# A hybrid decoder layer on one core: weight splits, bank choice and the second norm's sums at the borders of the up-projection

## The chip, the core and the metric

The kernel runs on one NeuronCore of a Trainium2 chip. The metric is the device time of one execution in microseconds (us). Before the change it is 923.74 us, the median of three runs (923.59 to 923.84).

The engines are TensorE (PE, with its weight loads listed as PEld), VectorE (DVE), ScalarE (ACT), GpSimd (POOL) and SyncE (SP), which issues most transfers. Matmuls write to PSUM, which has eight banks. A bank holds 512 fp32 values in each of 128 partitions.

## The reference, cut to what matters

One layer of a decoder, 1024 tokens of width 1024, in fp32:

```
z = rms_norm(h, norm_mix_g);  proj = z @ w_in            # pooling and recurrent heads follow
h = h + concat([y_pool, y_lru]) @ w_out
z = rms_norm(h, norm_mlp_g)                              # the second norm
h = h + square(relu(z @ w_up)) @ w_down                  # the MLP, 1024 -> 4096 -> 1024
z = rms_norm(h, norm_ple_g)
gate = sigmoid(z @ w_ple_gate + b_ple_gate)
h = h + gate * (p @ w_ple_proj)
return rms_norm(h, norm_final_g)
```

rms_norm divides by the root of the mean square over the 1024 channels and multiplies by a gain.

## The kernel before

**Products.** Channels lie on partitions, so the 1024 channels are eight tiles of 128, and tokens lie along the free dimension in two halves of 512. Every fp32 operand is split into a high part `hi` (rounded to fp32r) and the rest `lo`; `split` writes `hi` on ACT (line 185, or 188 with a gain) and `lo` on DVE (186, or 189). A product is three matmuls: hi by hi, hi by lo, lo by hi (line 363, in `mm`).

**The up-projection** is done in 16 pairs m = 0 to 15 by a seven-product scheme (P1 to P7) that combines quarter blocks of the weights and of the activations. Each product is 12 matmuls: four tiles t of the operand by three. P6 and P7 read the tiles `a` of indices 0 to 3, P4 and P5 those of indices 4 to 7, P1, P2 and P3 the tiles `y`. The operands with t = 3 need the last out-projection result (o = 7), so `up_first` runs t = 0 to 2 of P6, P7, P4, P5, and then their t = 3.

**Weights** are asked for through one list, `todo`. `ask()` takes the next entry, issues its loads and its split, and appends the result to `asked`; `weights()` asks once more and hands out the oldest. The up-projection's weights use four half-megabyte buffers in turn, so the fifth split has to wait until the matmuls of the first are done.

**The second norm.** `norm.acc` (T[4]) collects the squares of the eight tiles. `casts` splits it to `hl` tiles (420 on ACT, 421 on DVE); `sums` sends each half's hi and lo through a matmul with a matrix of ones (434, 435), and `rstd` makes 1/rms of the result (459 to 465). This is called inside pair m = 1, and pair 0 is finished by `finish_up` after it. The last norm of the kernel uses `folded` instead: rows 64 to 127 are copied by ACT beside rows 0 to 63 and added, hi goes to rows 0 to 63 of one tile and lo to rows 64 to 127, and one matmul with ones sums both (444 to 451).

**PSUM** is given out in two shapes: `bank` (four single banks, pool pd) and `banks` (two tiles of two banks, pool pp). `mlp_bank` and `psum` count their calls in `turn`: `mlp_bank` takes the two-bank shape at each third call, and `ple_psum`, in the gate stage, takes it at each odd count and otherwise two single banks, one for the gate `ps_e` and one for the projection `ps_j`. With the two-bank shape both halves are one tile, named `ps_e`.

**The end of the up-projection** is `up_last` (pair 15). It opens the down-projection's tiles, runs P4, P6, P7, and calls `prepare(0, tp)` for the four operand tiles of the first down product, which are splits of X[tp] into `a` on ACT and DVE.

**The last stage** works token by token in four groups of 128 tokens (i = 0 to 3). `gate_opened(i)` runs the gate's first matmul (1243) and adds the bias in PSUM on DVE (1252); `token_proj(i)` is six matmuls of the projection (1267); `token_gate(i)` is the other 23 of the gate, with the next group's first matmul after eleven of them. Tokens of the second half are transposed through DRAM (`turn` and `late`, lines 1198 to 1212) meanwhile.

**Order.** A scheduler in the framework orders each engine's instructions at build time, except those that are pinned by `pin` and `keep_in_program_order`. Each engine then runs its list in order.

Of the kernel before, what the change touches and what calls it, by code (L numbers as in the profile page):

```python
# [18 lines left out]
HALF = 512  # L19
# [44 lines left out]
def block_kernel(  # L64
# [67 lines left out]
    def bank(name):  # L132
        return pd.tile([P, HALF], F32, tag="pd", name=name)
# [19 lines left out]
    def f32(ap):  # L153
        return ap.bitcast(F32)
# [6 lines left out]
    def got(ps):  # L161
        if ps.shape[-1] > HALF:
            return ps.rearrange("p (b j a) -> p b a j", b=2, a=2)
        return ps.rearrange("p (j a) -> p a j", a=2)
# [177 lines left out]
    asked = []  # L342

    def ask():
        if todo:
            fn, *args = todo.pop()
            asked.append(fn(*args))

    def weights():
        ask()  # L350
        return asked.pop(0)
# [37 lines left out]
    class Norm:  # L389
# [47 lines left out]
                parts.append((hs, o))  # L437
            return parts

        def folded(self, hs, t):  # L440

            rows = self.acc[:, hs]
            x = rows[:64]
            nc.scalar.activation(t[:64], rows[64:], AF.Copy)
            nc.vector.tensor_tensor(x, x, t[:64], ALU.add)
            both, _ = self.parts(hs)
            hi, lo = (by(both[n], both) for n in (slice(0, 64), slice(64, P)))
            nc.vector.tensor_copy(hi, got(x))
            nc.vector.tensor_tensor(lo, got(x), f32(hi), ALU.subtract)
            o = bank(f"{self.name}_ps{hs.start}")  # L450
            nc.tensor.matmul(o, ones, turns(both), start=True, stop=True)
            return [(hs, o)]
# [355 lines left out]
    def mlp_bank(name):  # L808
        turn.append(name)
        return banks(name)[:, :HALF] if len(turn) % 3 == 0 else bank(name)  # L810
# [48 lines left out]
    leave("y2")  # L859
    *E, u0, u1 = space("wu", 4, F32, "right")  # L860
    up_spare += u0, u1
    for o in range(0, NT, 2):
        t = o // 2
        for i in range(2):
            split(H[o + i][:, FIRST], *half(B[t], i), col("g_mlp", o + i))
# [11 lines left out]
    def take(to, ps, y):  # L877

        nc.vector.tensor_tensor(by(to, ps), got(ps), by(y, ps), ALU.subtract)

    def up_first():
        cc, c11, c12, c21, c22 = up_sums(0)
        ps, ws = {}, {}
        ask()
        for kind in FIRST_UP[:4]:
            ws[kind], ps[kind] = weights(), mlp_bank(f"ps_{kind}_u0")
            up_product(0, kind, ps[kind], range(3), ws[kind])
        for kind in FIRST_UP[:4]:
            up_product(0, kind, ps[kind], range(3, 4), ws[kind])
        ws["P1"] = weights()  # L890
        with tc.issue_after(up_lower[0, "P1"]):
            up_second(NT - 1)
            norm.tmp = T[2:3]
            norm.add(H[NT - 1])
            copy(c22, ps["P5"])
            norm.casts()
        for kind in FIRST_UP[4:6]:
            ps[kind] = mlp_bank(f"ps_{kind}_u0")
            up_product(0, kind, ps[kind], w=ws.get(kind))
        up_product(0, "P3", ps["P5"], more=True)  # L900
        copy(c11, ps["P1"])
        take(c12, ps["P6"], c11)
        add_got(c21, ps["P7"], c12)
        add_got(c11, ps["P2"])
        dv(ALU.subtract, c22, c21, c22)
        add_got(c21, ps["P4"])
        take(c12, ps["P5"], c12)
# [22 lines left out]
    def up_pair(m):  # L930
        cc, c11, c12, c21, c22 = up_sums(m)
        a, d = up_open(m)
        b = chains[m]
        if m > 1:
            up_fourth(m - 1)()
        else:
            norm.rstd(R, norm.sums(cast=True))
            leave("hl")
        up_product(m, "P6", b, more=True)
        copy(c12, b)  # L940
        up_product(m, "P2", a, more=True)
        copy(c11, a)
        up_product(m, "P3", d, more=True)
        take(c12, d, c12)
        if m == 1:
            finish_up(0, up_sums(0)[0])()
        up_product(m, "P7", b, more=True)
        take(c22, b, c22)

    def up_last():  # L950
        m = NPAIR - 1
        cc, c11, c12, c21, c22 = up_sums(m)
        preload_down()
        a, d = up_open(m)
        store_up = up_fourth(m - 1)
        up_product(m, "P2", a, more=True)
        copy(c11, a)
        up_product(m, "P3", d, more=True)
        first = open_down()
        with tc.issue_after(first):  # L960
            store_up()
        ps = bank(f"ps_P4_u{m}")
        up_product(m, "P4", ps)
        load_w(0, 0, 3)
        copy(c21, ps)
        ps = bank(f"ps_P6_u{m}")
        up_product(m, "P6", ps)
        prepare(0, 0)
        take(c12, ps, c12)
        dv(ALU.subtract, c22, c12, c22)  # L970
        add(c21, c12)
        take(c12, d, c12)
        ps = banks(f"ps_P7_u{m}")[:, :HALF]
        up_product(m, "P7", ps)
        for tp in range(1, NQ):
            prepare(0, tp)
        add_both(cc[:, 1].rearrange("p (y s) -> p y s", y=2), ps)

    chains = {}

# [515 lines left out]
```

## Time and profile before

| | |
|---|---|
| median of three runs | 923.74 us (923.59 to 923.84) |
| the profiled execution's own time | 923.41 us |
| its span, first to last instruction | 921.6 us |
| busy: PE, PEld, DVE, ACT, POOL | 911.9, 792.9, 701.7, 468.9, 38.0 us |
| matmuls | 4227 |
| granted TensorE clock, mean | 0.998 |
| transfers | 142.46 MB, mean 155 GB/s |

Times in the views are us from the start of the span. A row of the timeline merges instructions of one kind that follow each other: start, length, engine, line, operation, output and input tiles, count, and in brackets the idle time before it with what ended it. The time outside the span is 923.41 - 921.6 = 1.8 us.

### The profile page before, as it was taken

The page shows a single profiled execution, that of the slowest core. Times are in us where ns is not written, and L with a number is a line of the kernel's source. Part 1 is how long each engine was busy: PE and PEld are TensorE (multiplying, and loading weights), DVE is VectorE, ACT ScalarE, POOL GpSimd, SP SyncE. Part 2 cuts the span into 40 slices and gives each one's busy share as a digit, 9 for nine tenths or more (in the row PEclk, how much of TensorE's full clock was granted, in tenths as well). Part 3 has the DMA queues.
Part 4 walks back from the last instruction along what each step waited for, and adds up shares of the span by engine and source line. Part 5 has one row for each costly group of instructions (what it writes and reads, how often), then busy time and mean ns, then how long its engine had stood idle before and what let it go on. Part 6 is the DMA issues. An engine that isn't in the chain of part 4 may idle for free.

```text
span 921.6 us, 11220 instructions
## 1 busy us (share of the span) xinstructions
PE 911.9 (99%) x4227; PEld 792.9 (86%) x4227; DVE 701.7 (76%) x850; ACT 468.9 (51%) x606; POOL 38.0 (4%) x54
## 2 busy tenths in 40 slices
PE   9999999999999999999999999999999999999996
PEld 7888888888888888888888888888888888888885
DVE  7998984668877566656766889899876679798766
ACT  6568992447554444445444654354343436656323
POOL 3400001000000000000000000000000000000001
PEclk9999999999999999999999999999999999999999
DMA  7211055214478767876864997466633351031453
GB/s 272 100 47 41 28 181 143 76 46 111 109 196 230 208 164 212 223 202 170 239 199 161 359 324 275 134 199 201 199 119 107 114 161 46 1 125 59 114 171 116
DMA packets 56870, 142.46 MB, mean 155 GB/s; under 512 B 4976, under 2 KB 9968, under 8 KB 56816
## 3 DMA queue, kind: packets, MB, share of 16 engines
q1 hardware_dynamic: 54080, 132.84, 44.2%
q0 software_dynamic: 2736, 8.91, 5.7%
q8 instruction: 33, 0.54, 0.3%
q14 instruction: 21, 0.17, 0.1%
HBM read 106.08 MB, written 35.65 MB: 154 GB/s over the span
## 4 chain that ended last, share of the span: by engine, by line
PE 93%; DVE 3%; issue 1%; DMA 1%; ACT 0%; SPq 0%; DVEq 0%; POOLq 0%; POOL 0%
PE ps_P_d L363 31%; PE ps_b_u L363 12%; PE ps_i L363 9%; PE ps_a_u L363 8%; PE ps_d_u L363 8%; PE ps_o L363 8%; PE ps_e L363 8%; PE ps_l L363 3%; PE ps_P_u L363 1%; PE ps_l L570 1%; PE ps_j L363 1%; DVE y L189 1%; PE ps_g L639 1%; PE ps_e L1243 1%; PE ps_p L363 1%
## 5 line engine op out<-in xcount | busy, mean ns | idle before, releaser
L363 PE MATMUL ps_P_d<-a,wd_P_hi 128*128 128x512 f32 x880 | 261.8, 379 | 0.0
L363 PEld LDWEIGHTS ps_P_d<-a,wd_P_hi 128*128 128x128 f32 x880 | 166.4, 189 | 23.5
L363 PE MATMUL ps_P_d<-a,wd_P_lo 128*128 128x512 f32 x440 | 166.8, 379 | 0.0
L363 PE MATMUL ps_b_u<-a,wu_P 128*128 128x512 f32 x504 | 113.5, 379 | 0.0
L363 PEld LDWEIGHTS ps_b_u<-a,wu_P 128*128 128x128 f32 x504 | 95.3, 189 | 13.5
L363 PEld LDWEIGHTS ps_P_d<-a,wd_P_lo 128*128 128x128 f32 x440 | 83.2, 189 | 11.8
L363 PE MATMUL ps_a_u<-y,wu_P 128*128 128x512 f32 x360 | 82.6, 379 | 0.0
L363 PEld LDWEIGHTS ps_a_u<-y,wu_P 128*128 128x128 f32 x360 | 68.1, 189 | 9.6
L820 DVE TENSOR_TENSOR t_h<-t_h,ps_P_d 128x512 f32<-128x512 f32 (+1 forms) x56 | 42.4, 758 | 36.7 <-PE ps_P_d L363 36.7
L186 DVE TENSOR_TENSOR a<-wd,a 128x1024 fp32r<-128x1024 f32 x56 | 67.0, 1217 | 0.9 <-ACT a L185 0.6
L363 PE MATMUL ps_i<-a,wi_hi 128*128 128x512 f32 x256 | 66.2, 381 | 0.0
L363 PE MATMUL ps_o<-y,wo_hi 128*128 128x512 f32 x256 | 65.7, 379 | 0.0
L185 ACT ACTIVATE a<-wd 128x1024 fp32r<-128x1024 f32 x56 | 57.9, 1048 | 7.0 <-PE ps_P_d L363 7.0
L363 PEld LDWEIGHTS ps_i<-a,wi_hi 128*128 128x128 f32 x256 | 48.1, 189 | 7.9 <-issue 1.0
L185 ACT ACTIVATE wd_P_hi<-wd 128x1024 fp32r<-128x1024 f32 x24 | 25.3, 1056 | 57.3 <-PE ps_P_d L363 57.2
L363 PEld LDWEIGHTS ps_o<-y,wo_hi 128*128 128x128 f32 x256 | 48.4, 189 | 6.8
L838 DVE SCALAR_TENSOR_TENSOR t_h<-t_h,rstd 128x2048 f32<-128x2048 f32 x16 | 36.7, 2291 | 19.3 <-ACT t_h L857 19.3
L186 DVE TENSOR_TENSOR wu_P<-wu,wu_P 128x512 fp32r<-128x512 f32 x47 | 32.3, 686 | 22.2 <-ACT wu_P L185 22.2
L186 DVE TENSOR_TENSOR wu_P<-wu_raw,wu_P 128x512 fp32r<-128x512 f32 x45 | 30.8, 687 | 23.6 <-ACT wu_P L185 23.6
L363 PE MATMUL ps_d_u<-a,wu_P 128*128 128x512 f32 x180 | 41.3, 379 | 0.0
L363 PE MATMUL ps_d_u<-y,wu_P 128*128 128x512 f32 x180 | 41.3, 379 | 0.0
L363 PEld LDWEIGHTS ps_d_u<-y,wu_P 128*128 128x128 f32 x180 | 34.0, 189 | 4.8
(265 smaller groups left out, 1541.5 us busy)
## 6 DMA issues: line engine op xcount, KB each, us to landing
wd<-act SPq DMA_DIRECT2D x56, 512.0 KB, 5.5
act<-t_h SPq DMA_DIRECT2D x32, 512.0 KB, 5.9
wu<-in_w_up SPq DMA_DIRECT2D x16, 512.0 KB, 4.8
act<-wu SPq DMA_DIRECT2D x16, 512.0 KB, 5.8
wd<-in_w_down SPq DMA_DIRECT2D x16, 512.0 KB, 7.0
wu_raw<-in_w_up SPq DMA_DIRECT2D x15, 512.0 KB, 5.7
t_h<-in_xT SPq DMA_DIRECT2D x14, 512.0 KB, 4.6
wg_raw<-in_w_gate SPq DMA_DIRECT2D x10, 512.0 KB, 3.2
```

What stands on the lines that cost most here:

```text
L185: first = pin(nc.scalar.activation(hi, src, AF.Copy))
L186: lowest[:] = [pin((eng or nc.vector).tensor_tensor(lo, src, f32(hi), ALU.subtract)).ins]
L189: lowest[:] = [pin(nc.vector.scalar_tensor_tensor(lo, src, g, f32(hi), ALU.mult, ALU.subtract)).ins]
L363: ins = nc.tensor.matmul(ps, w, turns(z[:, hs]), start=first and z is zhi and w is whi, stop=last and w is wlo, skip_group_check=more,)
L570: nc.tensor.matmul(ps, kblk(w, o), turns(z[:, hs]), start=k == n == 0, stop=False)
L639: nc.tensor.matmul(x, w[r, o * P : (o + 1) * P], turns(z[r, at : at + HALF]), start=n == 0, stop=n == 2)
L820: (eng or nc.vector).tensor_tensor(to, to if y is None else y, x, ALU.add)
L838: nc.vector.scalar_tensor_tensor(cc, cc, 0.0, twice(R), ALU.max, ALU.mult)
L1243: nc.tensor.matmul(pg, z, turns(quad[x == 1][:, k]), start=n == 0, stop=n == 3 * NT - 1, skip_group_check=True)
```

## The change

Three edits at the two borders of the up-projection, and the second norm's sums.

- At the opening, three weights (P7, P4, P5) are asked for ahead of the operand splits of `y`. P1's and P2's are asked for after the first four products.
- The second norm uses `fold` (lines 440 to 449 now, the first part of the old `folded`) with T[3] as scratch, in place of `casts`, and `folded` in place of `sums`.
- In `up_last` the three products take `mlp_bank` in place of `bank` and `banks`, and the preparation of X[1] to X[3] stands earlier.

```diff
-        def folded(self, hs, t):
+        def fold(self, hs, t):
             rows = self.acc[:, hs]
...
+        def folded(self, hs, t=None):
+            if t is not None:
+                self.fold(hs, t)
+            both, _ = self.parts(hs)
             o = bank(f"{self.name}_ps{hs.start}")
             nc.tensor.matmul(o, ones, turns(both), start=True, stop=True)
...
     up_spare += u0, u1
+    for _ in range(3):
+        ask()
     for o in range(0, NT, 2):
...
         ps, ws = {}, {}
-        ask()
         for kind in FIRST_UP[:4]:
-            ws[kind], ps[kind] = weights(), mlp_bank(f"ps_{kind}_u0")
+            ws[kind], ps[kind] = asked.pop(0), mlp_bank(f"ps_{kind}_u0")
             up_product(0, kind, ps[kind], range(3), ws[kind])
         for kind in FIRST_UP[:4]:
             up_product(0, kind, ps[kind], range(3, 4), ws[kind])
+        for _ in range(2):
+            ask()
         ws["P1"] = weights()
...
-            norm.casts()
+            for hs in HALVES:
+                norm.fold(hs, T[3][:, hs])
...
-            norm.rstd(R, norm.sums(cast=True))
+            norm.rstd(R, [x for hs in HALVES for x in norm.folded(hs)])
...
-        ps = bank(f"ps_P4_u{m}")
+        ps = mlp_bank(f"ps_P4_u{m}")
...
-        ps = bank(f"ps_P6_u{m}")
+        ps = mlp_bank(f"ps_P6_u{m}")
         up_product(m, "P6", ps)
-        prepare(0, 0)
+        for tp in range(2):
+            prepare(0, tp)
         take(c12, ps, c12)
+        ps = mlp_bank(f"ps_P7_u{m}")
+        up_product(m, "P7", ps)
+        for tp in range(2, NQ):
+            prepare(0, tp)
         dv(ALU.subtract, c22, c12, c22)
         add(c21, c12)
+        add_both(cc[:, 1].rearrange("p (y s) -> p y s", y=2), ps)
         take(c12, d, c12)
-        ps = banks(f"ps_P7_u{m}")[:, :HALF]
-        up_product(m, "P7", ps)
-        for tp in range(1, NQ):
-            prepare(0, tp)
-        add_both(cc[:, 1].rearrange("p (y s) -> p y s", y=2), ps)
```

**The opening on PE, before.** The matmuls of pair 0 ahead of P1's. The output's number is the product: 1777 is P6, 1790 P7, 1803 P4, 1816 P5.

```order
L363 MATMUL ps_P_u_1777<-a,wu_P_1671 128x512 x9
L363 MATMUL ps_P_u_1790<-a,wu_P_1767 128x512 x9
L363 MATMUL ps_P_u_1803<-a,wu_P_1774 128x512 x9
L363 MATMUL ps_P_u_1816<-a,wu_P_1787 128x512 x2
L363 MATMUL ps_P_u_1777<-a,wu_P_1671 128x512 x3
L363 MATMUL ps_P_u_1790<-a,wu_P_1767 128x512 x3
L363 MATMUL ps_P_u_1816<-a,wu_P_1787 128x512 x7
L363 MATMUL ps_P_u_1803<-a,wu_P_1774 128x512 x3
L363 MATMUL ps_P_u_1816<-a,wu_P_1787 128x512 x3
```

Now, with 1780 for P6, 1790 for P7, 1800 for P4, 1810 for P5:

```order
L363 MATMUL ps_P_u_1780<-a,wu_P_1671 128x512 x9
L363 MATMUL ps_P_u_1790<-a,wu_P_1745 128x512 x9
L363 MATMUL ps_P_u_1800<-a,wu_P_1752 128x512 x9
L363 MATMUL ps_P_u_1810<-a,wu_P_1755 128x512 x9
L363 MATMUL ps_P_u_1780<-a,wu_P_1671 128x512 x3
L363 MATMUL ps_P_u_1790<-a,wu_P_1745 128x512 x3
L363 MATMUL ps_P_u_1800<-a,wu_P_1752 128x512 x3
L363 MATMUL ps_P_u_1810<-a,wu_P_1755 128x512 x3
```

P6's last three (t = 3) were matmuls 30 to 32 and are 37 to 39; P5's first nine are no longer parted.

**The opening on DVE, now**, from P3's weight split to the first evacuations of pair 0 (`hl` are the second norm's split sums, 1874 and 1889 the weights P1 and P5 of pair 1, 1780 and 1790 the products P6 and P7 of pair 0):

```order
L186 TENSOR_TENSOR wu_P_1838<-rstd,wu_P_1838 128x512
L404 TENSOR_TENSOR t_h<-t_h 128x1024
L186 TENSOR_TENSOR wu_P_1874<-wu_1743,wu_P_1874 128x512
L445 TENSOR_TENSOR t_h<-t_h 64x512 x2
L448 CAST hl_134<-t_h 64x512
L448 CAST hl_135<-t_h 64x512
L449 TENSOR_TENSOR hl_134<-t_h,hl_134 64x512
L449 TENSOR_TENSOR hl_135<-t_h,hl_135 64x512
L186 TENSOR_TENSOR wu_P_1889<-wu_1744,wu_P_1889 128x512
L887 TENSOR_TENSOR t_h<-ps_P_u_1780,t_h 128x512
L218 TENSOR_TENSOR wu_1744<-wu_1744,wu_1743 128x512
L826 TENSOR_TENSOR t_h<-t_h,ps_P_u_1790 128x512
```

Six instructions stand where two of line 421 stood, and they stand behind P1's split of pair 1 instead of ahead of it. P5's split of pair 0, which was behind the two splits of `a`, is now ahead of them.

**The end of the up-projection on DVE, before**, from the first split of X (`a` from `wd`) on:

```order
L186 TENSOR_TENSOR a<-wd_3845,a 128x1024
L879 TENSOR_TENSOR t_h<-ps_P_u_3894,t_h 128x512
L186 TENSOR_TENSOR a<-wd_3846,a 128x1024
L218 TENSOR_TENSOR t_h<-t_h 128x512
L820 TENSOR_TENSOR t_h<-t_h 128x512
L186 TENSOR_TENSOR a<-wd_3847,a 128x1024
L879 TENSOR_TENSOR t_h<-ps_d_u_3755,t_h 128x512
L186 TENSOR_TENSOR a<-wd_3848,a 128x1024
```

Now:

```order
L186 TENSOR_TENSOR a<-wd_3847,a 128x1024
L186 TENSOR_TENSOR a<-wd_3848,a 128x1024
L887 TENSOR_TENSOR t_h<-ps_P_u_3896,t_h 128x512
L186 TENSOR_TENSOR a<-wd_3849,a 128x1024
L218 TENSOR_TENSOR t_h<-t_h 128x512
L186 TENSOR_TENSOR a<-wd_3850,a 128x1024
```

Two of the four combining steps that stood ahead of the last split of X stand behind it.

**The token stage on PE, before**, at i = 2 with what each waits for (DVE_49 is DVE's semaphore, Activation_49 ACT's):

```order
L1243 MATMUL ps_e_2_6628<-a 128x512 [waits Activation_49]
L1243 MATMUL ps_e_1_6584<-a 128x512 x12
L1267 MATMUL ps_e_2_6628<-proj_5935,proj_5931 128x512 [waits DVE_49]
L1267 MATMUL ps_e_2_6628<-proj_5936,proj_5931 128x512
L1267 MATMUL ps_e_2_6628<-proj_5935,proj_5932 128x512
L1267 MATMUL ps_e_2_6628<-proj_5937,proj_5933 128x512
L1267 MATMUL ps_e_2_6628<-proj_5938,proj_5933 128x512
L1267 MATMUL ps_e_2_6628<-proj_5937,proj_5934 128x512
L1243 MATMUL ps_e_2_6628<-a 128x512 x11
```

Now:

```order
L1254 MATMUL ps_e_2_6630<-a 128x512 [waits Activation_49]
L1254 MATMUL ps_e_1_6587<-a 128x512 x12
L1278 MATMUL ps_j_2_6631<-proj_5937,proj_5933 128x512
L1278 MATMUL ps_j_2_6631<-proj_5938,proj_5933 128x512
L1278 MATMUL ps_j_2_6631<-proj_5937,proj_5934 128x512
L1278 MATMUL ps_j_2_6631<-proj_5939,proj_5935 128x512
L1278 MATMUL ps_j_2_6631<-proj_5940,proj_5935 128x512
L1278 MATMUL ps_j_2_6631<-proj_5939,proj_5936 128x512
L1254 MATMUL ps_e_2_6630<-a 128x512 [waits DVE_49]
```

The three calls of `mlp_bank` add three to `turn`. The count's remainder by three is as before, so the down-projection's banks are the same, but its parity is turned: in the gate stage and the token stage the products that had a two-bank tile have two single banks, and the other way round. The wait for DVE's bias addition (1252) stood at the first matmul of the projection at i = 0 and i = 2; it stands now behind the projection there, at the gate's second matmul, and at the projection's first at i = 1.

## The prediction

> **What bounds the kernel now.** I read the page's busy line first, then PE's waits, then the chain of waits, then the timeline at each wait.
>
> ```profile
> PE 911.9 (99%) x4227; PEld 792.9 (86%) x4227; DVE 701.7 (76%) x850; ACT 468.9 (51%) x606; POOL 38.0 (4%) x54
> ...
> PE 93%; DVE 3%; issue 1%; DMA 1%; ACT 0%; SPq 0%; DVEq 0%; POOLq 0%; POOL 0%
> ```
>
> PE is busy for 99% and makes 93% of the chain. So a change can gain only where PE waits or where a matmul goes away. PE's waits are few:
>
> ```profile
> PE ps_e L1267 <- DVE ps_e L1252: 1.6, 2, 0.8
> PE ps_l L520 <- PEq L1482: 0.8, 1, 0.8
> PE ps_P_u L363 <- DVE wu_P L186: 0.4, 1, 0.4
> PE ps_P_d L363 <- DVE a L186: 0.2, 1, 0.2
> ```
>
> Three of the four lie where the change moves something: the opening of the up-projection (`ps_P_u`), its end (`ps_P_d`), and the token stage (`ps_e`, twice). A matmul's row is longer than its place, since they overlap, so losses are better counted in places:
>
> ```profile
> 244.53 2.59 PE ps_a_u L363 x12
> ```
>
> 12 matmuls take 2.59 us: 0.216 us each.
>
> **The opening of the up-projection.** PE, then DVE:
>
> ```profile
> 225.26 8.03 PE L363 MATMUL ps_P_u<-a,wu_P 128*128 128x512 f32 x35
> 233.68 3.07 PE L363 MATMUL ps_P_u<-a,wu_P 128*128 128x512 f32 x13 [0.39 <-DVE wu_P L186]
> 236.59 7.93 PE L363 MATMUL ps_P_u<-y,wu_P 128*128 128x512 f32 x36
> ...
> 230.68 2.34 DVE L186 TENSOR_TENSOR a<-t_h,a 128x1024 fp32r<-128x1024 f32 x2
> 232.95 0.67 DVE L186 TENSOR_TENSOR wu_P<-rstd,wu_P 128x512 fp32r<-128x512 f32 x1
> 234.15 0.74 DVE L189 SCALAR_TENSOR_TENSOR y<-t_h,y 128x512 fp32r<-128x512 f32 x1
> 234.82 0.68 DVE L186 TENSOR_TENSOR wu_P<-wu_raw,wu_P 128x512 fp32r<-128x512 f32 x1
> ...
> 236.14 0.63 ACT L185 ACTIVATE wu_P<-rstd 128x512 fp32r<-128x512 f32 x1 [2.12 <-PE ps_P_u L363]
> ```
>
> 48 matmuls ahead of P1 took 236.59 - 225.26 = 11.33 us, where 48 x 0.216 = 10.37 would do: 0.96 lost. After 29 matmuls PE needed the t = 3 operands (first `a` split, over at 231.85) and then P5's weights (split 232.95 to 233.62, behind both `a`). Now P5's split stands ahead of `a`, in the place of one `y` split of about the same length (0.67 from row to row), so `a` is not later. P5's nine come next, and t = 3 is wanted at 225.26 + 36 x 0.216 = 233.03, after 231.85; P4's t = 3 at 234.33, after the second `a` (233.0). Both waits go. What is late next is P1's weights: their buffer is P6's, free only when P6's last matmul (the 39th, started 233.47) has ended, 233.85. A split is 0.63 on ACT and 0.68 on DVE, so it is done at about 235.3. PE starts P1 at 225.26 + 10.37 = 235.63 and uses its `lo` two matmuls later. **Gain 0.96**; if the split ran 1 us late, 0.3 would be given back.
>
> **The second norm.** Each half's sums take one matmul for two: two of four go, 2 x 0.216 = **0.43**. They stand on PE between full products, so it counts in full. The price is on DVE and ACT. The last norm does one half this way:
>
> ```profile
> 866.24 0.68 DVE L445 TENSOR_TENSOR t_h<-t_h 64x512 f32<-64x512 f32 x1 [0.34 <-ACT t_h L444]
> 866.96 0.51 DVE L448 CAST sums<-t_h 64x512 fp32r<-64x512 f32 x1
> 867.51 0.83 DVE L449 TENSOR_TENSOR sums<-t_h,sums 64x512 fp32r<-64x512 f32 x1
> 868.37 1.23 DVE L186 TENSOR_TENSOR wg_lo<-wg_raw,wg_hi 128x1024 fp32r<-128x1024 f32 x1
> ...
> 865.58 0.63 ACT L444 ACTIVATE t_h<-t_h 64x512 f32<-64x512 f32 x1 [0.89 <-DVE t_h L404]
> ```
>
> One half is 868.37 - 866.24 = 2.13 us of DVE, two are 4.26 at most (3.6 if each overlaps the next by the 0.08 that neighbours do), against 1.66 before:
>
> ```profile
> 238.20 1.66 DVE L421 TENSOR_TENSOR hl<-t_h,hl 128x512 fp32r<-128x512 f32 x2 [0.70 <-ACT hl L420]
> 235.42 1.21 DVE L404 TENSOR_TENSOR t_h<-t_h 128x1024 f32<-128x1024 f32 x1
> 241.51 0.68 DVE L879 TENSOR_TENSOR t_h<-ps_P_u,t_h 128x512 f32<-128x512 f32 x1
> 242.11 0.68 DVE L218 TENSOR_TENSOR wu<-wu,wu 128x512 f32<-128x512 f32 x1
> 242.71 1.28 DVE L820 TENSOR_TENSOR t_h<-t_h,ps_P_u 128x512 f32<-128x512 f32 x2
> 246.95 2.75 PE L363 MATMUL ps_d_u<-a,wu_P 128*128 128x512 f32 x12
> ```
>
> Who waits behind it: P5's split of pair 1, then three steps, of which the third (first of L820) empties P7's bank. The program gives that bank to `ps_d_u` of pair 1. Before, it was empty at 243.4 and taken at 246.95. Now: P1's split ends 235.3, then `y` 0.67, two weight splits and the sum of squares (0.60, 0.60, 1.21) to 238.4, P1's split of pair 1 to 239.0, the fold of 3.6 to 4.3 to 242.6 to 243.3, the split and three steps (3 x 0.60 + 0.68) to 245.1 to 245.8. PE wants the bank 48 matmuls after P1's start, at 235.63 + 10.37 = 246.0. So it is hidden by 0.2 to 0.9 us; I take hidden, for ACT's share (two 0.63 rows) is paid beside DVE's queue. If the fold were 1 us dearer, up to 0.8 would be lost. What follows has more room: the sums are wanted at 248.6, 5 us after the fold.
>
> The Trainium skill (VectorE: DVE Perf Modes, section Two Vector instructions with no wait between them) speaks against this edit: an instruction whose output starts in another group of 32 partitions than the last one's starts only when all before it have finished. The fold's `lo` rows go to partitions 64 to 127. The one such row agrees: L449 is 0.83 and the next starts 0.86 after it, without the usual overlap. By the rule the fold lies at the 4.3 end, with 0.2 of room, and the sum stays; another 0.2 and the first rival's wait begins.
>
> **The end of the up-projection.**
>
> ```profile
> 517.17 4.48 PE L363 MATMUL ps_P_d<-a,w 128*128 128x512 f32 x19
> 521.83 1.35 PE L363 MATMUL ps_P_d<-a,w 128*128 128x512 f32 x5 [0.17 <-DVE a L186]
> 523.01 0.59 PE L363 MATMUL ps_P_d<-a,wd_P_hi 128*128 128x512 f32 x2
> ...
> 514.75 1.22 DVE L186 TENSOR_TENSOR a<-wd,a 128x1024 fp32r<-128x1024 f32 x1
> 515.89 0.68 DVE L879 TENSOR_TENSOR t_h<-ps_P_u,t_h 128x512 f32<-128x512 f32 x1
> 520.56 1.21 DVE L186 TENSOR_TENSOR a<-wd,a 128x1024 fp32r<-128x1024 f32 x1
> ```
>
> The first down product's 24 matmuls took 523.01 - 517.17 = 5.84 us against 24 x 0.216 = 5.18: 0.66 lost, waiting for the third and fourth split of X. The fourth starts 520.56 - 514.75 = 5.81 after the first: three splits (1.14 each) and four steps of 0.60. Now two of those steps are behind it: 5.81 - 1.20 = 4.61, over at 4.61 + 1.21 = 5.82 after the first split's start. Everything here shifts alike, so that is 3.40 after PE's start of this product, and PE wants it at its 20th matmul, 19 x 0.216 = 4.10 after. It is in time by 0.7: **gain 0.66**. The steps now behind it (L820, L879) feed `finish_up`, whose stores are read products later. The bank count changes nothing here, since the evacuations stand in the same places.
>
> **The token stage.** It follows from the parity of the bank count.
>
> ```profile
> 886.69 0.38 PE L1243 MATMUL ps_e<-a 128*128 128x512 f32 x1
> 887.86 1.56 PE L1267 MATMUL ps_e<-proj,proj 128*128 128x512 f32 x6 [0.79 <-DVE ps_e L1252]
> 901.86 1.56 PE L1267 MATMUL ps_e<-proj,proj 128*128 128x512 f32 x6 [0.79 <-DVE ps_e L1252]
> 903.26 2.10 PE L1243 MATMUL ps_e<-a 128*128 128x512 f32 x9
> ...
> 887.11 0.70 DVE ps_e L1252
> 891.02 2.62 DMA turn<-late
> 893.72 4.27 DMA late<-turn
> 901.20 0.62 DVE ps_e L1252
> ```
>
> At groups 0 and 2 the projection waits for the bias addition, though it writes the tile's other bank. Each costs what lies beyond the places: 887.86 - 886.69 - 0.216 = 0.95, and 0.10 more behind the restart (six places are 1.30, and 903.26 - 901.86 is 1.40): 1.05 each. Now the projection has its own bank there and runs ahead. At group 0 the gate's second matmul comes 7 places (1.51) after the first, and the addition is over 887.81 - 886.69 = 1.12 after it: hidden, gain 1.05. At group 2 the addition is late for another reason: DVE stands in its queue behind work on `late` that returns from DRAM. From group 0's first matmul (886.69) to the end of that addition (901.82) are 15.13 us, which no edit shortens. PE has 67 places to the gate's second matmul of group 2, 14.47, so it waits about 0.7. That matmul comes at 15.13 + 0.04 after 886.69, 901.86 in old terms, where it was at 903.26: **gain 1.40 in all**, bounds 2.10 (no chain) and 0 (the chain 1.4 longer). At group 1, now on the two-bank tile, the projection comes 12 places (2.59) after the gate's first matmul, longer than the addition's 1.12: no wait.
>
> In the gate stage the parity turns too. A product there is 24 matmuls (5.2 us), and PE waits for no bank before it now, so I take nothing.
>
> **Sum.** 0.96 + 0.43 + 0.66 + 1.40 = 3.45 us. The profiled execution took 923.41 (span 921.6), 0.33 under the median. From the median: 923.74 - 3.45 = 920.3 us.
>
> **The rivals.**
> - *The fold is the new wait.* `ps_d_u` of pair 1 waits for P7's bank. For it: 0.2 to 0.9 us of room and the longest DVE rows one behind the other. Against it: all steps are from rows. With 4.3 and half a us of hand-over more, 0.3 to 0.8 is lost: 920.9 us.
> - *The token stage gives nothing*, as the DRAM chain is then what sets the pace: transfers that come 1.4 us later (two of them make 6.9 of the 15.13) eat the gain. 923.74 - 2.05 = 921.7 us.
> - *The borders' waits come back with another operand* (P1's buffer, a transfer of X): the change doesn't do what it says there. The 0.96 and 0.66 go: 923.74 - 1.83 = 921.9 us, no change that can be told.
> - *Slower.* The same chain through DRAM in the token stage: once it alone sets group 2, each us that it lengthens is a us. It decides from 3.45 on, that is at 15.13 + 3.45 = 18.6 us, both transfers half as long again. With 5.5 longer: 925.8 us. For it: the change leaves that chain no cover. Against it: no transfer is added, or moved against its neighbours.
>
> **How the numbers follow.** Forecast 0.62, fold 0.12, token stage 0.10, borders 0.10, slower 0.04; the last 0.02 is a gain over 4 us. The range takes the bound of 0.7 us more in the token stage on one side (919.6) and the token and border rivals on the other (921.9): 919.5 to 921.9. A measurement of this kernel tells about 0.2%, 1.85 us, from no change, so faster means below 921.9: forecast, fold, most of the token rival and part of the borders', 0.82. Same 0.14, slower 0.04.
>
> **What would show it.** Right: PE's waits list no `ps_P_u` and no `ps_P_d`; P1 of pair 0 starts 10.4 us after the first `ps_P_u`; two `n_ps` matmuls with `hl` there, and `ps_d_u` of pair 1 follows without a gap; only one wait for L1252's successor, of about 0.7 us, at the gate in group 2. Wrong: a gap ahead of `ps_d_u` of pair 1, a wait for `a` in the first down product, or a token stage that is as long as before from group 0's first gate matmul on.

## The result, and the profile after

The changed kernel takes 918.51 us (median of four runs, 918.35 to 919.26) against 923.66 us for the kernel before on the same chip (four runs, 923.13 to 923.84): a ratio of 0.9947, 95% interval 0.993 to 0.9964. That is 5.15 us less, where 3.45 were forecast. The profiled execution took 918.40 us, with a span of 916.6; before it was 923.41 and 921.6.

The page's busy line, its chain line, and the whole list of PE's waits (us in total, times, longest):

```profile
PE 909.1 (99%) x4225; PEld 792.0 (86%) x4225; DVE 703.8 (77%) x854; ACT 468.6 (51%) x606; POOL 38.9 (4%) x54
...
PE 98%; issue 1%; DVE 0%; DVEq 0%; ACT 0%; POOLq 0%; POOL 0%
```

```profile
PE ps_l L526 <- PEq L1493: 0.8, 1, 0.8
```

The waits at the opening, at the end of the up-projection and in the token stage are gone and nothing took their place: of the chain that ends last, DVE has 0% where it had 3%, and DMA is no longer listed. Two matmuls fewer were issued. PE's timeline at the opening, the norm and the end of the up-projection:

```profile
224.42 10.52 PE L363 MATMUL ps_P_u<-a,wu_P 128*128 128x512 f32 x48
234.78 7.93 PE L363 MATMUL ps_P_u<-y,wu_P 128*128 128x512 f32 x36
...
245.14 2.75 PE L363 MATMUL ps_d_u<-a,wu_P 128*128 128x512 f32 x12
247.73 0.59 PE L457 MATMUL n_ps<-hl,ones 128*128 128x512 f32 x2
...
514.93 5.34 PE L363 MATMUL ps_P_d<-a,w 128*128 128x512 f32 x24
520.11 0.59 PE L363 MATMUL ps_P_d<-a,wd_P_hi 128*128 128x512 f32 x2
```

All 48 matmuls ahead of P1 stand in one row: 234.78 - 224.42 = 10.36 us for 11.33. `ps_d_u` of pair 1 begins where its place is (10.36 after P1), two `n_ps` matmuls follow it for four, and the first down product's 24 matmuls are one row too, 5.18 us for 5.84. The token stage, on PE:

```profile
883.79 0.38 PE L1254 MATMUL ps_e<-a 128*128 128x512 f32 x1
884.01 1.46 PE L1278 MATMUL ps_j<-proj,proj 128*128 128x512 f32 x6
885.30 5.34 PE L1254 MATMUL ps_e<-a 128*128 128x512 f32 x24
...
896.96 1.46 PE L1278 MATMUL ps_j<-proj,proj 128*128 128x512 f32 x6
898.25 1.03 PE L1254 MATMUL ps_e<-a 128*128 128x512 f32 x4
```

From group 0's first gate matmul to group 2's second: 898.25 - 883.79 = 14.46 us for 903.26 - 886.69 = 16.57. There is no wait at group 2, where 0.7 us was forecast. The whole account, from the two profiled executions:

| stretch on PE | before | after | difference | forecast |
|---|---|---|---|---|
| start to the first `ps_P_u` | 225.26 | 224.42 | -0.84 | none |
| opening of the up-projection | 11.33 | 10.36 | -0.97 | -0.96 |
| `ps_d_u` of pair 1 to the first down product (the second norm's matmuls, four and now two, are in it) | 270.22 | 269.79 | -0.43 | -0.43 |
| first down product | 5.84 | 5.18 | -0.66 | -0.66 |
| token stage, as above | 16.57 | 14.46 | -2.11 | -1.40 |
| the rest | | | 0.0 | 0 |
| span | 921.6 | 916.6 | -5.0 | -3.45 |

So two questions are left: why the token stage gave 0.71 us more, and what the 0.84 us at the start are, in a part of the program that the change doesn't touch.

### The profile page after: what moved, and what is told of

Read it like the earlier page. It is cut to its first block, busy times and chain, and to the rows that moved or that the text cites. A ratio compares the mean times of both kernels' runs of the same rounds, so it can differ in the third digit from the quotient of the medians.

```text
span 916.6 us, 11225 instructions
## 1 busy us (share of the span) xinstructions
PE 909.1 (99%) x4225; PEld 792.0 (86%) x4225; DVE 703.8 (77%) x854; ACT 468.6 (51%) x606; POOL 38.9 (4%) x54
## 4 chain that ended last, share of the span: by engine, by line
PE 98%; issue 1%; DVE 0%; DVEq 0%; ACT 0%; POOLq 0%; POOL 0%
PE ps_P_d L363 32%; PE ps_b_u L363 12%; PE ps_i L363 9%; PE ps_o L363 9%; PE ps_d_u L363 8%; PE ps_a_u L363 8%; PE ps_e L363 8%; PE ps_l L363 3%; PE ps_P_u L363 3%; PE ps_e L1254 2%; PE ps_l L576 1%; PE ps_j L363 1%; PE ps_g L645 1%; PE ps_p L363 1%; PE ps_l_second L363 1%
## 5 line engine op out<-in xcount | busy, mean ns | idle before, releaser
L185 ACT ACTIVATE wu_P<-wu 128x512 fp32r<-128x512 f32 x47 | 29.3, 625 | 21.1 <-PE ps_b_u L363 14.0
```

Of the source, the lines that this page charges most:

```text
L185: first = pin(nc.scalar.activation(hi, src, AF.Copy))
```

## The experiments

Each single edit was timed alone, then the two disputed things were pulled apart. All ratios are to the kernel before on the same chip in the same set of runs.

**The opening alone.**

```diff
+    for _ in range(3):
+        ask()
     for o in range(0, NT, 2):
...
-            ws[kind], ps[kind] = weights(), mlp_bank(f"ps_{kind}_u0")
+            ws[kind], ps[kind] = asked.pop(0), mlp_bank(f"ps_{kind}_u0")
...
+        for _ in range(2):
+            ask()
         ws["P1"] = weights()
```

> The kernel before with only the opening's edit: three weight splits ahead of the y splits, two more behind the four products. The 48 matmuls from the first ps_P_u to the first ps_P_u<-y took 11.33 us before and 10.36 in the full change. Theory 'the order alone does it': 10.36 here, -0.97 us, about 922.7 us. Rival 'it needs the cheaper queue that the norm edit leaves behind it' (DVE has the old casts, 1.66 us in place of 3.81): then the wait comes back at P1 or later and less than 0.5 us is gained. Separately, the very start: the first ps_P_u stood at 225.26 in the profile before and at 224.42 in the full change, with the same program up to there. Theory 'the start varies from execution to execution': either number can show here, and it moves together with the first matmuls of L570 (5.35 us or less than 4.9 us for the first of the seven). Rival 'the change does it through its build': 224.4 shows only in kernels with the edit that causes it.

Measured: 922.46 us for 923.46, ratio 0.9991 (0.9982 to 1.0001). One row of 48 matmuls, 235.30 - 224.94 = 10.36 us:

```profile
224.94 10.52 PE L363 MATMUL ps_P_u<-a,wu_P 128*128 128x512 f32 x48
235.30 7.93 PE L363 MATMUL ps_P_u<-y,wu_P 128*128 128x512 f32 x36
...
901.05 1.56 PE L1270 MATMUL ps_e<-proj,proj 128*128 128x512 f32 x6 [1.26 <-DVE ps_e L1255]
```

The order alone does it, -0.97 on PE; the time alone would not tell it from no change, as its interval reaches 1.0001. The start is neither 224.4 nor 225.3, so it varies from execution to execution. It does not move with the first L570 matmuls alone, as was expected: these run as in the change (from 4.34, the seven in 1.51 us), and PE then waits for an operand. With the restart that is the 0.52 us by which 224.94 lies above the change's 224.42:

```profile
9.39 1.97 PE L570 MATMUL ps_l<-a,wl_hi 128*128 128x512 f32 x8 [0.28 <-DVE a L512]
```

The last row of the view before that is of the token stage, which this kernel has as before: its wait for group 2's bias addition is 1.26 us, where the profile before has 0.79. That wait varies too.

**The fold alone**, in the second norm: `norm.fold` for `norm.casts`, `folded` for `sums`.

```diff
-            norm.casts()
+            for hs in HALVES:
+                norm.fold(hs, T[3][:, hs])
...
-            norm.rstd(R, norm.sums(cast=True))
+            norm.rstd(R, [x for hs in HALVES for x in norm.folded(hs)])
```

> The kernel before with only the second norm's sums by folded rows. Theory 'two matmuls go, the DVE work is hidden': two n_ps matmuls with hl in place of four, ps_d_u of pair 1 still without a gap, -0.43 us, about 923.2 us. Rival 'the fold is a new wait' (its DVE rows take 3.81 us in the full change, 2.2 us more than the old casts): a gap of 0.2 to 0.8 us ahead of ps_d_u of pair 1, since here the opening's wait of 0.39 us still delays DVE's queue by nothing and PE by 0.96; gain then 0.2 or nothing.

Measured: 922.18 us for 923.46, ratio 0.9987 (0.9977 to 0.9996). `ps_d_u` of pair 1 has no gap (246.81, 10.36 after P1's 236.45) and the norm has two matmuls, so the fold is hidden. The median is 1.28 us down, though the two matmuls make 0.43. This profile's token stage took 15.52 us in place of 16.57, without the change of banks, so the kernel was run again:

> The kernel before with only the second norm's fold, once more, since its median of 922.18 us lay 1.28 us under before's where two matmuls are worth 0.43, and its profile had the token stage at 15.52 us in place of 16.57. Theory 'uneven chain through DRAM': the median comes back to -0.4 to -0.9 us against before, and the token stage of this profile lies anywhere from 15.5 to 17.0. Rival 'the fold shortens the token stage too': 15.52 again, and -1.3 us again.

Measured: 922.40 us for 923.75, ratio 0.9987 (0.9979 to 0.9996). In this profile the token stage took 16.98 us:

```profile
885.94 0.38 PE L1250 MATMUL ps_e<-a 128*128 128x512 f32 x1
887.11 1.56 PE L1274 MATMUL ps_e<-proj,proj 128*128 128x512 f32 x6 [0.79 <-DVE ps_e L1259]
...
901.52 1.56 PE L1274 MATMUL ps_e<-proj,proj 128*128 128x512 f32 x6 [1.19 <-DVE ps_e L1259]
902.92 0.38 PE L1250 MATMUL ps_e<-a 128*128 128x512 f32 x1
```

The same program takes 15.52 us in one execution and 902.92 - 885.94 = 16.98 in another: the fold doesn't shorten this stage. The expected return of the median to -0.4 to -0.9 failed, however: it is 1.35 us down again. Both intervals hold 0.43, but two medians 0.9 us beyond it are not explained by any row.

**The order of splits and combining steps alone**, at the end of the up-projection, with the banks counted as before.

```diff
-        prepare(0, 0)
+        for tp in range(2):
+            prepare(0, tp)
         take(c12, ps, c12)
-        dv(ALU.subtract, c22, c12, c22)
-        add(c21, c12)
-        take(c12, d, c12)
         ps = banks(f"ps_P7_u{m}")[:, :HALF]
         up_product(m, "P7", ps)
-        for tp in range(1, NQ):
+        for tp in range(2, NQ):
             prepare(0, tp)
+        dv(ALU.subtract, c22, c12, c22)
+        add(c21, c12)
         add_both(cc[:, 1].rearrange("p (y s) -> p y s", y=2), ps)
+        take(c12, d, c12)
```

> The kernel before with only the order of the splits and combining steps at the end of the up-projection, banks counted as before. Theory 'the order alone does it': 24 matmuls of the first down product in 5.18 us where 5.84 stood, -0.66 us, about 923.0 us; the token stage from group 0's first gate matmul (L1243) to group 2's second keeps 16.57 us. Rival 'the bank count is part of it' (P4, P6 and P7 on other banks let the evacuations come sooner): less than 0.3 us here and the rest only with the count.

Measured: 922.68 us for 923.46, ratio 0.9991 (0.9982 to 1.0001).

```profile
516.49 5.34 PE L363 MATMUL ps_P_d<-a,w 128*128 128x512 f32 x24
521.67 0.59 PE L363 MATMUL ps_P_d<-a,wd_P_hi 128*128 128x512 f32 x2
```

521.67 - 516.49 = 5.18 us: the order alone gives the 0.66, the banks have no part in it.

**The parity alone.** Three entries more in the count turn its parity and keep it modulo three.

```diff
+        turn.extend(["none"] * 3)
         ps = bank(f"ps_P4_u{m}")
         up_product(m, "P4", ps)
         load_w(0, 0, 3)
```

> The kernel before with three more entries in the count of banks ahead of the last up-projection pair's P4: the count modulo three stays, its parity turns, so that only the gate and token stages take their banks the other way round. In the token stage, from group 0's first gate matmul to group 2's second, 16.57 us before and 14.46 in the full change. Theory 'the chain through DRAM is not 15.13 us but what its transfers make of it' (its first read back took 4.27 us in the profile before and 3.2 in the full change, 14.28 us for the whole chain there): 14.46 us where the chain is below 14.46, and longer by the excess where the transfers are slow, so between -2.1 and -1.4 us. Rival 'the chain always takes 15.13 us at this parity too and something else of the full change shortens it': 15.1 to 15.2 us, -1.40. Rival 'banks in the gate stage matter too': a change ahead of 886.69, where none is expected (0.0).

Measured: 921.04 us for 923.46, ratio 0.9977 (0.9967 to 0.9986), the largest of the four.

```profile
886.39 0.38 PE L1244 MATMUL ps_e<-a 128*128 128x512 f32 x1
886.61 1.46 PE L1268 MATMUL ps_j<-proj,proj 128*128 128x512 f32 x6
...
899.56 1.46 PE L1268 MATMUL ps_j<-proj,proj 128*128 128x512 f32 x6
900.86 1.46 PE L1244 MATMUL ps_e<-a 128*128 128x512 f32 x6
```

900.86 - 886.39 = 14.47 us, and the projection (now `ps_j`, on its own bank) runs ahead at groups 0 and 2. The parity alone gives the token stage's whole gain, and no other edit of the change is needed for it. From the first `ps_P_u` to group 0's first gate matmul it is 661.44 us (886.39 - 224.95) for 661.43 before, so the turned banks change nothing in the gate stage.

**The changed kernel again**, unedited.

> The changed kernel once more, for a second profile of it and more times. Theory 'the chain through DRAM is of uneven length': in six profiles so far group 2's bias addition started 13.21 to 14.89 us after group 0's first gate matmul; the changed order hides it up to about 13.8, so this profile shows 14.46 us to group 2's second gate matmul if the start is below 13.8, and longer by the excess if it is above. Theory 'the start is uneven': first ps_P_u between 224.4 and 225.3. The times then lie some 1 us apart, against 2.0 us (922.25 to 924.28) for the 30 of before, since the old order lets every length above 13.5 through. Rival 'the change itself shortens chain and start': 224.42 and 13.58 again, to a few hundredths.

Measured: 919.08 us (918.92 to 919.50) for 923.41, ratio 0.9955 (0.9943 to 0.9968): 4.33 us less, against 5.15 in the first four runs. The first `ps_P_u` stands at 225.43 in this profile, later than before's 225.26, and the token stage is 14.46 again. So the 0.84 us at the start is not the change's. Without the start, the profiles of the change give 4.16 us (from the first `ps_P_u` to the end, 916.6 - 224.42 = 692.18, against 696.34 before) and 4.07 (917.7 - 225.43 = 692.27).

**Group 2's bias addition taken off the chain through DRAM.** On DVE it now stands ahead of the two additions that wait for the rows read back (the output's transfer is held behind the last read, so that SP's order stays).

```diff
         opened = token_gate(i, pg)
+        if i == 1:
+            early(0)
         sigmoids(i, pg)
...
         if i == 0:
-            for x in range(2):
-                early_square(x)
-                early_gain(x)
+            continue
         mean(i)
```

`early(0)` holds the lines that are taken out, with the mean and the inverse of group 0. In the kernel before:

> The same move of group 2's bias addition in the kernel before, with its banks as they were. It takes the chain away but not the projection's wait for the addition at group 0 (1.05 us). Theory 'two independent parts': 15.52 us from group 0's first gate matmul to group 2's second (16.57 in the profile before, 14.46 with the banks turned), so -0.7 us in the median at least (the chain's waits of 0 to 1.5 us go, and the 1.05 of group 0 stays), about 922.6 us. Rival 'the bank order is all of it': no change, 923.5 us, group 2's wait in place.

Measured: 922.18 us for 923.41, ratio 0.9986 (0.9977 to 0.9995).

```profile
886.49 0.38 PE L1245 MATMUL ps_e<-a 128*128 128x512 f32 x1
887.66 1.56 PE L1269 MATMUL ps_e<-proj,proj 128*128 128x512 f32 x6 [0.79 <-DVE ps_e L1254]
...
900.72 1.46 PE L1269 MATMUL ps_e<-proj,proj 128*128 128x512 f32 x6
902.01 2.32 PE L1245 MATMUL ps_e<-a 128*128 128x512 f32 x10
```

902.01 - 886.49 = 15.52 us: with the old banks group 0's wait stays and group 2's goes with the chain. These are two separate causes, as the forecast had it. In the changed kernel:

> The changed kernel, with group 2's bias addition on DVE ahead of the two additions that wait for the rows back from DRAM (L1242) instead of behind them and the mean. It no longer hangs on that chain: its start comes some 11 us after group 0's first gate matmul, 14.46 us to group 2's second gate matmul whatever the transfers take. Theory 'uneven chain, mostly hidden by the change': the same median as the change (within 0.3 us), fewer long executions. Rival 'the change leaves a wait in many executions': 0.3 us or more under it. Rival 'what stands behind on DVE comes late': a wait at group 3 or a longer end, 0.3 us or more over it.

Measured: 919.08 us (918.98 to 919.47), ratio 0.9955 (0.9943 to 0.9968), 14.46 us in the token stage: the same as the change without it. So the change leaves little of that wait in a usual execution.

**The chain made longer** in the changed kernel, by one DVE instruction.

```diff
                 early_gain(x)
+            x = quarter(1, 0)
+            pin(nc.vector.tensor_tensor(x, x, x, ALU.max))
         mean(i)
```

> The changed kernel with one DVE instruction of 128x512 more (a maximum of the rows with themselves, which leaves them as they are) on the chain through DRAM, between the early additions and the mean: 0.61 us more ahead of group 2's bias addition. Theory 'the change hides the chain up to a start at about 13.8 us, with 0.2 us to spare in its profile': PE waits at group 2's second gate matmul by what start + 0.65 is above 14.46, that is 0.4 us at a chain as in the change's profile (13.58 + 0.61 = 14.19), from 0.0 (13.21 + 0.61 = 13.82) to 1.7. In the median 0.3 to 0.7 us over the change. Rival 'the chain is not what group 2 waits for': no wait, the same time.

Measured: 920.15 us (919.53 to 920.33), ratio 0.9966 (0.9952 to 0.9979); 1.07 us over the change in the same set, more than the 0.3 to 0.7 expected. DVE, then PE:

```profile
897.24 0.69 DVE L1417 TENSOR_TENSOR late<-late 128x512 f32<-128x512 f32 x1
...
898.52 0.69 DVE L1263 TENSOR_TENSOR ps_e<-ps_e,t_h 128x512 f32<-128x512 f32 x1
...
897.73 1.46 PE L1278 MATMUL ps_j<-proj,proj 128*128 128x512 f32 x6
899.27 0.92 PE L1254 MATMUL ps_e<-a 128*128 128x512 f32 x3
```

The gate's matmul follows the addition's start by 899.27 - 898.52 = 0.75 us, and comes 14.70 us after group 0's first (884.57): the wait that the forecast placed at group 2 is real. The size is not accounted for. The added instruction puts 0.61 us on the chain, and whatever wait a longer chain makes beyond that, the change has too. So by this wait the two kernels can differ by 0.61 at most, not by 1.07. The rest is unexplained; with five executions of each, the two intervals overlap (0.9952 to 0.9979 here, 0.9943 to 0.9968 for the change).

**The fold made dearer** in the changed kernel.

```diff
             for hs in HALVES:
+                x = norm.acc[:, hs]
+                nc.vector.tensor_tensor(x, x, x, ALU.max)
                 norm.fold(hs, T[3][:, hs])
```

> The changed kernel with one DVE instruction of 128x512 more ahead of each half's fold (a maximum of the sums of squares with themselves, which leaves them as they are). The planner, which sees them, also puts one weight split of pair 1 ahead of the step that empties P7's bank: three rows more, 1.8 us, stand before that step. In the change's profile the step began at 243.77 and ps_d_u of pair 1 at 245.14; with 0.75 us from a step's start to the matmul that it releases (as in the token stage) there were 0.62 us to spare. Theory 'the fold hides behind the bank of P7': PE now waits 1.8 - 0.62 = 1.2 us ahead of ps_d_u of pair 1, 0.5 if one of the rows fills a gap that DVE has anyway, and the time is 0.5 to 1.2 us longer. Rival 'P7's bank is not what DVE's queue is late for': no gap, the same time as the change. Rival 'the fold's length is paid in full somewhere': 1.8 us and more.

Measured: 921.12 us for 923.75, ratio 0.997 (0.996 to 0.9979). PE's waits, then DVE and PE:

```profile
PE ps_d_u L363 <- DVE t_h L826: 1.4, 1, 1.4
...
PE ps_e L1256 <- DVE ps_e L1265: 0.3, 1, 0.3
```

```profile
247.14 1.28 DVE L826 TENSOR_TENSOR t_h<-t_h,ps_P_u 128x512 f32<-128x512 f32 x2
...
247.88 1.35 PE L363 MATMUL ps_d_u<-a,wu_P 128*128 128x512 f32 x5 [1.45 <-DVE t_h L826]
```

The wait is at P7's bank, where the prediction's first rival put it. P1 began at 235.91, so the place of `ps_d_u` was 246.27, and it came at 247.88: 1.61 us late. DVE's step came 11.23 us after P1's start, where it was 8.99 in the change (243.77 - 234.78), and 2.24 later less 0.62 of room makes the 1.62. Three rows (1.8 us) and a gap of 0.45 us for ACT's copies make up the 2.24. The wait is above the 0.5 to 1.2 us that were expected, since that sum had no term for the gap. The times can't settle its size: the change was not run in this set, and 923.75 - 921.12 = 2.63 us is 1.7 to 2.5 less than the change gained in its own sets, which would fit the rival of 1.8 us and more as well. The profile puts 1.61 at the bank and 0.45 (14.91 - 14.46) in the token stage. In this execution the chain through DRAM was long enough to show as well (0.3 us in the second row).

**Folding the third norm too**, in the changed kernel, then with the moved bias addition:

```diff
-                    norm2.casts((FIRST,))
+                    norm2.fold(FIRST, T[1][:, FIRST])
...
-        norm.rstd(R, norm.sums((FIRST,), cast=True))
+        norm.rstd(R, norm.folded(FIRST))
...
-                    norm2.rstd(R, norm2.sums((SECOND,)))
+                    norm2.rstd(R, norm2.folded(SECOND, T[2][:, SECOND]))
```

> The changed kernel with the third norm's two halves folded as well: one matmul for two in each half, 2 x 0.216 = 0.43 us less on PE; on DVE two additions, two casts and two subtractions of 64x512 more against one cast and two subtractions of 128x512 less. Theory 'a matmul between full products counts in full and the fold hides': -0.43 us against the change, profile with n_ps and n2b_ps of one matmul each. Rival 'here the fold is late': rstd of the third norm is awaited by the gate's operands, a wait ahead of a gate matmul, the gain gone or 0.5 us lost.

Measured: 918.82 us for 923.75, ratio 0.9945 (0.9933 to 0.9956).

```profile
811.44 0.38 PE L457 MATMUL n_ps<-sums,ones 128*128 128x512 f32 x1
825.90 0.38 PE L457 MATMUL n2b_ps<-sums,ones 128*128 128x512 f32 x1
```

One matmul for two in each half. From the first `ps_P_u` to group 0's first gate matmul it is 658.94 us (884.61 - 225.67), where the change has 659.37: the 0.43. The token stage lost 0.18 of it to a chain whose addition started at 13.89.

> The changed kernel with both additions together: the third norm folded (its profile: 0.43 us less from the first ps_P_u to group 0's first gate matmul) and group 2's bias addition ahead of the chain through DRAM. With the third norm's fold alone group 2's addition started 13.89 us after group 0's first gate matmul and its second gate matmul at 14.64 in place of 14.46; here 14.46 whatever the transfers take. Theory: from the first ps_P_u to the end 692.18 - 0.43 = 691.75 us in the profile, 0.4 to 0.7 us under the change in the median, about 918.4 us, and executions less far apart than 1 us but for the start. Rival 'what stands behind the moved addition comes late': a wait at group 3, no gain over the change.

Measured: 918.77 us (918.48 to 919.13) for 923.38, ratio 0.9951 (0.9937 to 0.9964), the token stage at 14.46. Its profile has 916.7 - 224.92 = 691.78 us from the first `ps_P_u` to the end, 0.40 less than the change. The ratios of this version, of the third norm's fold alone and of the change can't be told apart: the gain is shown in PE's places, not in the medians.

## Why the prediction was right and wrong

The direction and three of four terms hold to 0.01 us: the opening, the norm and the first down product. They were counts of matmuls by a place of 0.216 us, and each was reproduced on PE by its edit alone. The fold was hidden, with 0.62 us of room where 0.2 to 0.9 were worked out; its six DVE rows took 241.96 - 238.15 = 3.81 us, between the 3.6 and 4.3 given:

```profile
238.15 1.29 DVE L445 TENSOR_TENSOR t_h<-t_h 64x512 f32<-64x512 f32 x2
239.36 0.94 DVE L448 CAST hl<-t_h 64x512 fp32r<-64x512 f32 x2
240.34 1.59 DVE L449 TENSOR_TENSOR hl<-t_h,hl 64x512 fp32r<-64x512 f32 x2
241.96 0.69 DVE L186 TENSOR_TENSOR wu_P<-wu,wu_P 128x512 fp32r<-128x512 f32 x1
...
243.77 1.28 DVE L826 TENSOR_TENSOR t_h<-t_h,ps_P_u 128x512 f32<-128x512 f32 x2
```

The second of the two L449 by itself:

```profile
241.09 0.83 DVE L449 TENSOR_TENSOR hl<-t_h,hl 64x512 fp32r<-64x512 f32 x1
```

The rule of the Trainium skill on held instructions (VectorE: DVE Perf Modes, section Two Vector instructions with no wait between them) was weighed against this edit, and these rows agree with it. Where the output moves to other partitions nothing overlaps: the first L449 starts at 240.34, after the casts are over (239.36 + 0.94 = 240.30), and the split behind the second starts at 241.96, after that one is over (241.93). Where it stays, neighbours overlap: the second L449 starts at 241.09, and the first runs to 241.17. The prediction put the fold at the 4.3 end, twice the rows of one half, in which the output moves four times in all; in the order of the change, both halves' rows of a kind together, it moves twice. By the rule, that is part of why the fold is 3.81 us.

The forecast time was 1.8 us too long, and 918.51 lies 1.0 below the range's lower end. Two things failed. The first, with 2.11 in place of 1.40, brings the sum to 923.74 - 4.16 = 919.6 us, 0.1 inside the range's end; the second, 0.84 us at the start that no term held, takes it below, to 918.7. That these 0.84 fell on the side of the gain was luck, but not all of the miss is: in its second set of runs the change took 919.08 us, also under the range.

**The token stage's term: 1.40 forecast, 2.11 measured.** The mechanism was right: the projection's wait at group 0 goes, and group 2's matmul follows the addition behind the rows from DRAM wherever that addition is late. What failed is the step "15.13 us, which no edit shortens": that was the length of one execution, taken as a constant. Across the profiles group 2's addition started so long after group 0's first gate matmul, and group 2's second gate matmul followed:

| kernel | banks | addition starts | second gate matmul |
|---|---|---|---|
| before | old | 14.42 | 16.57 |
| opening alone | old | 14.89 | 17.04 |
| order of splits alone | old | 14.36 | 16.51 |
| fold alone, twice | old | 13.21, 14.83 | 15.52, 16.98 |
| changed, twice | turned | 13.58, 13.70 | 14.46, 14.46 |
| parity alone | turned | 13.61 | 14.47 |
| third norm folded | turned | 13.89 | 14.64 |
| fold dearer | turned | 14.16 | 14.91 |
| chain longer by 0.61 | turned | 13.95 | 14.70 |

Every row follows one of two rules. With the banks turned, the gate's matmul comes at 14.46 or 0.75 after the addition's start, whichever is later. With the old banks the projection comes first, behind the addition, so it is 15.52, or the start + 0.75 + 1.40. At one and the same chain, then, the change is worth 1.06 to 1.40 us, and at before's 14.42 exactly the 1.40 of the forecast. The other 0.71 is that the chain was 0.84 us shorter in the profile after (13.58) than in the one before; the last 0.13 of the 0.84 only add to the cover. The starts with old banks average 14.34, those with turned banks 13.71 (the last row's less 0.61), and they overlap (13.21 to 14.89 and 13.34 to 14.16). Part of that may belong to the banks: ACT's square of the second read-back starts 11.19 to 12.06 us after group 0's first gate matmul in all eight profiles with turned banks, and at 12.27 to 12.80 in five of six with the old ones (11.11 in the sixth). The medians of the set with the moved addition point the same way: taking the addition off the chain was worth 923.41 - 922.18 = 1.23 us with the old banks and 919.08 - 919.08 = 0.00 with the turned ones. By the two rules, chains of one length could make these two differ by 13.71 - 13.37 = 0.34 at most, so by these medians the chain was about 0.9 us longer in the kernel before. But the medians of the fold alone lie as far from what its rows explain, and by what path banks of PSUM would act on these transfers no run shows. So it stays open how much of the 0.71 is the change's and how much one execution's. SP's transfers come at the same times in both up to the first read (7.0 us after group 0's first gate matmul); from there the two read-backs land differently:

```profile
894.01 0.63 ACT L1238 ACTIVATE t_h<-late 128x512 f32<-128x512 f32 x1 [2.73 <-DMA late<-turn]
...
895.27 0.63 ACT L1238 ACTIVATE t_h<-late 128x512 f32<-128x512 f32 x1 [0.54 <-DMA late<-turn]
```

That is 10.22 and 11.48 us after group 0's first gate matmul in the change, and 11.32 and 12.33 before.

**The start, 0.84 us, in no term.** It is not the change's: in fourteen profiles, of kernels whose PE runs the same matmuls up to there, the first `ps_P_u` stands anywhere from 224.42 (the profile after) to 225.67. The forecast compared single executions and medians of three, and gave its range no width for that. PE's first matmuls, before and then after:

```profile
4.37 0.77 PE L570 MATMUL ps_l<-a,wl_hi 128*128 128x512 f32 x1
4.92 0.63 PE L570 MATMUL ps_l<-a,wl_lo 128*128 128x512 f32 x1
5.35 2.01 PE L570 MATMUL ps_l<-a,wl_hi 128*128 128x512 f32 x7
7.20 0.81 PE L570 MATMUL ps_l<-a,wl_lo 128*128 128x512 f32 x3
```

```profile
4.34 0.45 PE L576 MATMUL ps_l<-a,wl_hi 128*128 128x512 f32 x1
4.63 0.38 PE L576 MATMUL ps_l<-a,wl_lo 128*128 128x512 f32 x1
4.85 1.67 PE L576 MATMUL ps_l<-a,wl_hi 128*128 128x512 f32 x7
6.36 0.81 PE L576 MATMUL ps_l<-a,wl_lo 128*128 128x512 f32 x3
```

The same nine matmuls take 7.20 - 4.37 = 2.83 us and 6.36 - 4.34 = 2.02. The first go at about half the later rate (0.43 us from one to the next, 0.216 later), and the full rate begins at about 6.0 in the one (the seven from 5.35 to 7.20 are 0.34 longer than 7 x 0.216, one to two slow ones) and about 4.6 in the other. That is 0.81 of the 0.84. The granted clock reads 1.00 in both in each microsecond from 0 to 10, so that column doesn't show it. The Trainium skill (TensorE: Matmul & The Clock Gate, Part 1: The HAM clock gate) describes such a phase, says that its end depends on a window that runs free of the kernel's start, and that it varies from run to run; the rows agree. In four of the fourteen profiles later L570 matmuls come another 0.2 to 0.8 us late, in two of them (the opening alone, and the fold alone in its first profile) behind waits for operands that the profile lists. In the other ten it is 217.41 us from the twelfth matmul behind the first L570 to the first `ps_P_u`, each time.

**The rivals.** The fold as a new wait did not come true, but its place was right, as the dearer fold shows: with 2.24 us more ahead of the step, PE waited at P7's bank. That the token stage gives nothing, and that the borders' waits come back, fell with the rows above. Two of the rivals, the token stage that gives nothing and the slower case, charged a longer chain to the change alone. By the two rules above, the old banks pay for it too, us for us from 13.37 us on, and at any one length the change keeps 1.06 to 1.40 us; no chain came near the 18.6 us either.

## What to carry to other kernels

Terms that are counts of matmuls by a place came out to 0.01 us; the one that contained a write to DRAM and a read back came out by how long these took that time. A length through DRAM that stands in one profile should be carried as a range (here 13.2 to 14.9 us for the same work), and so should the first few microseconds of PE. Where a wait is set by such a chain, order the work so that the chain has cover at its long end: the old banks covered an addition that starts up to 13.37 us (15.52 - 2.15), the turned ones up to 13.71 (14.46 - 0.75), and at 13.89 a wait of 0.18 was back.

## What the runs showed of the hardware that was not expected

- The first matmuls run at half rate until about 4.6 us into the span in one execution and 6.0 in another, which makes 0.8 us between them (0.43 us from one to the next against 0.216), while the granted clock is given as 1.00.
- The first of the two 256 KB reads from DRAM, issued 6.98 to 7.06 us after group 0's first gate matmul in every profile, let ACT begin 9.63 to 11.79 us after that matmul. SP's issue of the two reads took 0.82 us in nine profiles and 1.88 to 2.19 in five, all five with turned banks; the issue of the two writes behind them took 0.92 to 2.69. What holds an issue was not tried.
- From a DVE addition's start in PSUM to the first matmul that waits for it are 0.75 us, for a row of 0.69 (899.27 - 898.52, and 247.88 - 247.14 with the step that empties P7's bank: 0.74).
